# Soft mixture of experts by nested fast matrix products: more pairs split a third time

## The chip, the cores and the metric

The kernel runs on one core of one Trainium2 chip. The metric is the device time of one execution in microseconds (us); lower is better. The time before is the median of three runs. The profile is of one more execution, taken by the hardware profiler.

## The reference

```python
x: (16, 512, 512)   router_logits: (16, 512, 8)   expert_weights: (8, 512, 2048)   all float32
probs = softmax(router_logits, axis=-1)
output = zeros((16, 512, 2048))
for e in range(8):
    output += probs[:, :, e:e+1] * matmul(x, expert_weights[e])
```

With the probabilities multiplied into x this is one product of an 8192 x 4096 matrix (tokens by expert and hidden index) and a 4096 x 2048 matrix (the weights).

## The kernel before

**The products.** The big product is cut 2 x 2 x 2 and made by Winograd's form of Strassen's scheme, with seven products instead of eight; the code calls them P1 to P7 (`right[r]`, `lefts[r, q]`, `products[r, q]`). P1 takes the first four experts' weights and the first half of the output columns (`b11`), P2 the last four experts' (`b21`); the right sides of P3 to P7 are sums of weights. Rows come in 16 blocks q of two times 256. Each `Product` is cut once more in the same way, into seven steps in the order `STEPS = (1, 5, 6, 2, 7, 3, 4)`. A step is eight matmuls of 128 x 128 by 128 x 512 (f16 into a PSUM bank of f32). Its inputs are, on the left, `z` (x times a probability, made by VectorE; halves 0 and 1 of the inner index), `s2` (pool `d`) and the inner `i`; on the right blocks of weights (1, 2, 3) and sums of them (5, 6, 7, 4), tiles of pool `w`. After a step `post` takes its bank: P1's results go by ScalarE copies and VectorE adds to `kept` in DRAM; P2 fetches these as a base into a tile of pool `h`, and VectorE adds the bank to it at every step but step 2.

**The split.** `Split` and `Third` cut steps 1 and 5 of a pair of products (a and b, two neighbouring row blocks) a third time. The two steps of both products would be 4 x 8 = 32 matmuls of 512 columns; as a third level they are 2 x 7 parts (named x1 to x7 for step 1, q1 to q7 for step 5) of four matmuls of 256 columns, 56 in all. For it VectorE makes four sums S of the lefts for each pair (`Third.queue_sums`, tile `s`: 128 x 1024), eight sums `t` of the weights once for each r (`Split.queue`; 128 x 1024), and adds halves of banks after parts 6 and 7 (128 x 256). ScalarE copies half of a bank after part 5, and the other half into `t5`. x5 needs the first sum S0, x6 S1, and so on.

**The stages.** `stages` is a list of one or two products that TensorE works through step by step, a and b in turn; a stage of two has 14 slots. Stages 0 to 5 are P1's pairs (q = 2 to 13), stages 6 and 7 hold one product of P2 and one of P1, stages 8 to 14 are P2's pairs, and stage 15 (`k5`) begins P5. Before stage 0 a first phase makes P1's rows q = 0 and 1 directly: for two column halves n, four experts e, four chunks c and four row parts j it runs one matmul each, with weights as they land; `early_z0` and `early_xp1` make its inputs and those of stage 0 by matmuls with a diagonal, and `keep_p` stores all probabilities in `p_dram`. Where the next stage is split, the last two slots (step 4 of a and b) are held and run between its parts (`held`, `run_third`): x1 x5 q1 q5, a held slot, x2 q2 x6 q6, the other, x7 q7 x3 q3 x4 q4.

**The order.** Each engine runs in the order in which the program names its work (`keep_in_program_order`). VectorE's work that nobody needs at once lies in `queue` as `Task`s with costs. `slack()`, called at each slot, adds 1.73 us to TensorE's planned clock and runs tasks while VectorE's planned clock is at least 0.3 us behind; `need(task)` runs the queue up to a task that a step requires, wherever it stands; `evacuated()` adds what `post` costs. A stage's own inners come into the queue when it starts (`queue_i`), the next stage's lefts, S, s2 after its first slot (`queue_lefts`). Hooks (`at(stage, slot, ...)`) start the rest: `fetch_at` the bases on SyncE's queue, `wedge_at` the casts and three sums that prepare later right sides (12 and 22), `odd_t` and `sums_at` more of these. `start_loads(stage + 2)` puts the next but one stage's `xT` and `pT` on SyncE's queue after slot 1, or after the slot that `late` names. Stores of results go by GpSimd's queue, weights that return from DRAM (`fetch_w`) by ScalarE's.

**The pools.** `w` has 15 tiles, `z` 8, `x` 9, `h` 13, `d` 3, PSUM 8 banks. A tile is handed out again when its last reader is done; a DMA or an engine that writes into it waits for that.

Before the change stages 2 to 5 and 9 are split, and six of P3's. The weight sums `t` of P1 are queued in stage 1, those of P2 in stage 8.

Of the kernel before, what the change touches and what calls it, by code (L numbers as in the profile page):

```python
# [31 lines left out]
def kernel(  # L32
# [7 lines left out]
    nc = tc.nc  # L40
    P = 128
# [35 lines left out]
    def half():  # L77
        return h_tile([P, NB], f32)
# [32 lines left out]
    def tt(o, a, b, op):  # L111
        dve(nc.vector.tensor_tensor(out=o, in0=a, in1=b, op=op))  # L112
# [9 lines left out]
    def sp(o, i):  # L122
        note(nc.sync.dma_start(out=o, in_=i))
# [7 lines left out]
    def mm(ps, z, w, start, stop):  # L131
        note(nc.tensor.matmul(ps, z, w, start=start, stop=stop, skip_group_check=True))  # L132
# [3 lines left out]
    def new_w():  # L136
        return wpool.tile([P, K8, NB], f16, name="w", tag="w")
# [31 lines left out]
    def inner_sums(b, t7=None):  # L169

        w = {1: b[0, 0], 2: b[1, 0], 3: b[1, 1], 7: t7 or b[0, 1]}

        def step(p, x, y):
            if p not in w:
                w[p] = new_w()
            tt(w[p], x, y, SUB)
        return w, {5: lambda: step(5, b[0, 1], b[0, 0]), 6: lambda: step(6, b[1, 1], w[5]),
                   4: lambda: step(4, b[1, 0], w[6]), 7: lambda: step(7, b[1, 1], b[0, 1])}
# [39 lines left out]
    def early_p(t):  # L218
        if t == 0:
            return softmax(lg0[t], 4, cpool.tile([P, HE, 4], f16, name="ph0"))  # L220
        pf = softmax(lg0[t], 4, cpool.tile([P, HE, 4], f32, name="pf0"))
        odd = pf.rearrange("p e (q j) -> p e q j", j=2)[:, :, :, 1]
        tt(odd[:, 0:2], odd[:, 0:2], odd[:, 2:4], ADD)
        ph = cpool.tile([P, HE, 4], f16, name="ph1")
        dve(nc.vector.tensor_copy(ph, pf))
        return ph
# [16 lines left out]
    def diag_e(e):  # L243
        return diag(ph0[0][:, e].unsqueeze(2))

    def early_z0(e, d, js=range(4)):
        for j in js:
            ps = bank()
            for c in range(C):
                mm(ps[:, ds(c * P, P)], xs0[:, j, ds(c * P, P)], d[:, j], c == 0, c == C - 1)  # L250
            evacuate(z0[j][:, e], ps.rearrange("p (c t) -> p c t", c=C), j)
# [8 lines left out]
    def early_xp1(j, d):  # L260
# [6 lines left out]
        mm(ps, ones, d.rearrange("p e t -> p (e t)"), True, True)  # L267
        evacuate(xp1[t][1][:, :, rows], ps.rearrange("p (e t) -> p e t", e=HE), 1)

    R = 4  # L270
    J = HQ // R
    p_dram = dram.tile([NHQ, 3 * HE, HQ], f16, name="p_dram")
# [32 lines left out]
                for c in (2 * g, 2 * g + 1) for j in (2 * h, 2 * h + 1)]  # L305
    ORDERS = [(c, j) for c in range(C) for j in range(4)], QUARTERS

    ds_ = [diag_e(0)]
    early_z0(0, ds_[0], (0, 1))
    for i in range(3):  # L310
# [4 lines left out]
    for e in (1, 2):  # L315
        ds_.append(diag_e(e + 1))
        early_z0(e, ds_[e])
    for n in range(2):
        ps = [bank() for _ in range(4)]
        for e in range(HE):  # L320
            if n == 0 and e == 1:
                early_z0(3, ds_[3])
                ph0.append(early_p(1))
                ds_ = [diag_j(j) for j in range(4, 8)]
                keep_p = softmax_of_all()
                w, sums = inner_sums(b11, new_w())
            for c, j in ORDERS[n == 0 and e == 0]:
                mm(ps[j], z0[j][:, e, c], b11[e // 2, n][:, e % 2 * C + c, :],
                   e + c == 0, e == HE - 1 and c == C - 1)
            if n == 1:  # L330
                for j in ((4, 5), (6, 7), (), ())[e]:
                    early_xp1(j, ds_[j - 4])
                if e == 1:
                    sums[5]()
        for j in range(4):
            o = half()
            act(nc.scalar.copy(o, ps[j]))
            sp(kept[j // 2][n].rearrange("(p j) m -> j p m", j=2)[j % 2], o)
        if n == 0:
            keep_p()  # L340

    ordered[0] = True
# [247 lines left out]


    THIRD = (1, 5)
    COLS = [ds(i * HQ, HQ) for i in range(2)]

    class Split:

# [8 lines left out]

        def make(self, p, i):
            if i == 0:
                self.t[p] = wpool.tile([P, 4, C, HQ], f16, name="t", tag="w")
            w, t = self.right.op(p), self.t[p]
            block = lambda k, n: w[:, ds(k * C, C), COLS[n]]  # L610
            x, y = ((block(0, 1), block(0, 0)), (block(1, 1), t[:, 0]), (block(1, 1), block(0, 1)),
                    (block(1, 0), t[:, 1]))[i]
            tt(t[:, i], x, y, SUB)

        def op(self, p, m):
            if m in (1, 2, 3):
                k, n = ((0, 0), (1, 0), (1, 1))[m - 1]
                return self.right.op(p)[:, ds(k * C, C), COLS[n]]
            i = {5: 0, 6: 1, 7: 2, 4: 3}[m]
            need(self.task[p, i])  # L620
            return self.t[p][:, i]

    class Third:
# [25 lines left out]
        def part(self, p, m):  # L649
            n = "xq"[THIRD.index(p)]  # L650
            if m == 1:
                self.b.banks[n] = bank()
            ya, yb = self.a.banks.get(n), self.b.banks[n]
            z, w = self.op(p, m), self.split.op(p, m)
            o = {1: (yb, 0), 5: (yb, 1), 2: (ya, 0), 6: (yb, 0), 7: (yb, 0), 3: (ya, 1), 4: (yb, 0)}[m]
            for c in range(C):
                mm(o[0][:, COLS[o[1]]], z[:, c], w[:, c], m == 1 and c == 0, c == C - 1)
            clock["pe"] += 0.44
            if m == 5:
                ya = self.a.banks[n] = bank()  # L660
                act(nc.scalar.copy(ya[:, COLS[0]], yb[:, COLS[0]]))
                self.t5[n] = h_tile([P, HQ], f32)
                act(nc.scalar.copy(self.t5[n], yb[:, COLS[1]]))
            elif m in (6, 7):
                evacuated(0.35)
                tt((ya if m == 6 else yb)[:, COLS[1]], yb[:, COLS[0]], self.t5[n], ADD)

# [262 lines left out]
    for q in range(1, 13, 2):  # L930
        add(product(3, q), product(3, q + 1))
    end = add(product(3, 13))
    late[k3 - 1] = 6

    for k, q in ((k7, 14), (k7 + 1, 15)):
        at(k - 1, 6, lambda q=q: queue_into(lefts[7, q]))
# [76 lines left out]
    sums_at(5, 8, 2, b21, (7,))  # L1013
    sums_at(5, 12, 2, b21, (4,))
    for i, (kn, e) in enumerate((kn, e) for kn in ((0, 0), (1, 0), (1, 1)) for e in range(2)):
        wedge_at(4 + i, 2, kn, e, (4 + i, 11))

    def fetch_at_w(stage, slot, of, what, kn):
        at(stage, slot, lambda: of.__setitem__(kn, fetch_w(what, kn)))
# [43 lines left out]
    last2 = k5 - 1  # L1063
    for stage, slot, q in ((9, 9, 12), (10, 2, 11), (10, 9, 22), (last2, 8, 21)):
        at(stage, slot, lambda q=q: cast_odd(q))
    at(11, 6, odd_t)
    for i, kn in enumerate(((0, 0), (1, 1), (1, 0))):
        fetch_at_w(11 + (8 + 4 * i) // 14, (8 + 4 * i) % 14, t1, "t1", kn)
        fetch_at_w(last2, 2 + 2 * i, t2, "t2", kn)
    sums_at(12, 8, 5, t1, (5, 6))  # L1070
    sums_at(13, 2, 5, t1, (7, 4))
    sums_at(last2, 9, 6, t2, (5, 6))
    at(k5, 4, odd_t4)
    sums_at(k5, 5, 6, t2, (7, 4))
# [141 lines left out]
            post(p)  # L1216
    finish.step, finish.post = step_at_end, post_at_end

    for stage in (2, 3, 4, 5):
        third(stage, 1)  # L1220
    at(1, 2, splits[1].queue)
    for stage in (9, ):
        third(stage, 2)
    at(8, 2, splits[2].queue)

    for q in KEEP:
        for k, slot in enumerate((1, 5)):
# [3 lines left out]
        third(stage, 3)  # L1231
    at(k3, 9, splits[3].queue)

    need_first = [right[1].task[p] for p in (6, 7, 4)]
    for p in (2, 3):
        lefts[1, p].queue_make(0)
    queue.append(need_first[0])
    for p in (2, 3):
        lefts[1, p].queue_s2()
    for p in (2, 3):  # L1240
        lefts[1, p].queue_make(1)
    queue.extend(need_first[1:])
    start_loads(1)
    store_loads(0)
    finish_loads(1)
# [30 lines left out]
```

## Time and profile before

| What | Value |
|---|---|
| Median of three runs | 1366.98 us (1366.88 to 1367.12) |
| Profiled execution, its own time | 1367.07 us |
| Its span, first to last instruction | 1365.1 us |
| Granted TensorE clock | 1.000 |
| TensorE (PE) busy | 1359.9 us, 100% |
| VectorE (DVE) busy | 1126.5 us, 83% |
| GpSimd (POOL) busy | 407.0 us, 30% |
| ScalarE (ACT) busy | 195.7 us, 14% |
| DMA | 356.41 MB, mean 261 GB/s |

The profile's rows read so: engine, line of the code, operation, the tile written `<-` the tiles read, sizes, and a count; a timeline row begins with its start and its length in us, and ends with the engine's idle time before it and who ended it. A row of a stretch of time gives for each engine its busy time (and instructions), then the granted clock, the share of the DMA engines and GB/s. Most calls pass through helpers: line 132 is every matmul, 112 every VectorE tensor-tensor operation, 123 SyncE's DMAs and 126 GpSimd's, so that rows are told apart by their tiles. Matmuls overlap, so their mean duration (375 ns) is longer than their spacing.

### The profile page before, as it was taken

The page shows a single profiled execution, that of the slowest core. Times are in us where ns is not written, and L with a number is a line of the kernel's source. Part 1 is how long each engine was busy: PE and PEld are TensorE (multiplying, and loading weights), DVE is VectorE, ACT ScalarE, POOL GpSimd, SP SyncE. Part 2 cuts the span into 40 slices and gives each one's busy share as a digit, 9 for nine tenths or more (in the row PEclk, how much of TensorE's full clock was granted, in tenths as well). Part 3 has the DMA queues.
Part 4 walks back from the last instruction along what each step waited for, and adds up shares of the span by engine and source line. Part 5 has one row for each costly group of instructions (what it writes and reads, how often), then busy time and mean ns, then how long its engine had stood idle before and what let it go on. Part 6 is the DMA issues. An engine that isn't in the chain of part 4 may idle for free.

```text
span 1365.1 us, 18194 instructions
## 1 busy us (share of the span) xinstructions
PE 1359.9 (100%) x6657; PEld 648.7 (48%) x6657; DVE 1126.5 (83%) x1367; ACT 195.7 (14%) x362; POOL 407.0 (30%) x644
## 2 busy tenths in 40 slices
PE   9999999999999999999999999999999999999998
PEld 4455544544444444444444444444444444456554
DVE  5975787989789788788887888888889797998873
ACT  3232311100011111111111100000000000123221
POOL 3123333331223342333322122242332422223232
PEclk9999999999999999999999999999999999999999
DMA  9999999999898999999999978989898979999896
GB/s 195 242 218 228 253 242 323 310 300 383 257 304 268 311 350 274 293 279 292 328 258 331 344 247 221 216 240 203 232 252 220 252 203 292 302 217 245 196 206 119
DMA packets 193385, 356.41 MB, mean 261 GB/s; under 512 B 53136, under 2 KB 87184, under 8 KB 188176
## 3 DMA queue, kind: packets, MB, share of 16 engines
q0 software_dynamic: 88048, 183.02, 55.3%
q1 hardware_dynamic: 99488, 132.25, 31.9%
q10 hardware_dynamic: 5760, 39.99, 7.6%
q8 instruction: 52, 0.85, 0.2%
q14 instruction: 37, 0.30, 0.1%
HBM read 214.47 MB, written 167.97 MB: 280 GB/s over the span
## 4 chain that ended last, share of the span: by engine, by line
PE 99%; DMA 0%; DVE 0%; issue 0%; ACT 0%; POOLq 0%
PE ps L132 99%; DMA w<-in_x_dram 0%; DVE z L238 0%; DVE h L112 0%; ACT h L1213 0%; POOLq L1260 0%
## 5 line engine op out<-in xcount | busy, mean ns | idle before, releaser
L132 PE MATMUL ps<-w,z 128*128 128x512 f16 x5240 | 1125.7, 375 | 0.0
L132 PEld LDWEIGHTS <-z 128*128 128x128 f16 x5328 | 521.2, 98 | 598.4
L126 POOL DMA_DIRECT2D out_dram<-h x380 | 249.3, 662 | 736.5 <-ACT h L582 352.6
L112 DVE TENSOR_TENSOR h<-ps,h 128x512 f32<-128x512 f32 x415 | 284.6, 687 | 184.7 <-PE ps L132 166.7
L112 DVE TENSOR_TENSOR z<-xT,pT 128x2048 f16<-128x2048 f16 x216 | 261.9, 1217 | 0.0
L132 PE MATMUL ps<-w,d 128*128 128x512 f16 x880 | 199.1, 379 | 0.0
L132 PEld LDWEIGHTS <-d 128*128 128x128 f16 x880 | 86.1, 98 | 101.5
L112 DVE TENSOR_TENSOR z<-z,d 128x2048 f16<-128x2048 f16 x110 | 131.7, 1217 | 0.0
L582 ACT COPY h<-ps 128x512 f32<-128x512 f32 x64 | 37.5, 585 | 524.5 <-PE ps L132 521.1
L112 DVE TENSOR_TENSOR w<-w 128x1024 f16<-128x1024 f16 (+2 forms) x88 | 100.0, 1146 | 1.8 <-PE ps L132 1.0
L571 ACT COPY h<-ps 128x512 f32<-128x512 f32 x90 | 52.7, 585 | 293.5 <-PE ps L132 264.1
L112 DVE TENSOR_TENSOR ps<-ps,h 128x512 f32<-128x512 f32 (+1 forms) x110 | 64.0, 585 | 26.0 <-PE ps L132 25.7
L112 DVE TENSOR_TENSOR d<-z 128x1024 f16<-128x1024 f16 x110 | 74.6, 687 | 5.1 <-PE ps L132 3.6
L568 ACT COPY h<-ps 128x512 f32<-128x512 f32 x90 | 51.8, 589 | 132.4 <-PE ps L132 129.6
L126 POOL DMA_DIRECT2D kept<-h x56 | 30.8, 549 | 110.9 <-ACT h L571 78.0
L126 POOL DMA_DIRECT2D wd<-w x78 | 44.2, 592 | 35.0 <-DVE w L112 27.5
L126 POOL DMA_DIRECT2D w<-in_expert_weights_dram x65 | 48.6, 778 | 19.5 <-issue 13.8
L112 DVE TENSOR_TENSOR u<-xT,pT 128x2048 f16<-128x2048 f16 x38 | 46.2, 1217 | 0.0
L112 DVE TENSOR_TENSOR h<-h 128x512 f32<-128x512 f32 (+2 forms) x69 | 45.1, 675 | 0.1
L112 DVE TENSOR_TENSOR z<-z,u 128x2048 f16<-128x2048 f16 x34 | 41.3, 1216 | 0.1
L112 DVE TENSOR_TENSOR z<-z 128x2048 f16<-128x2048 f16 x32 | 39.1, 1222 | 0.7
L564 ACT COPY ps<-ps 128x512 f32<-128x512 f32 x45 | 25.6, 570 | 94.4 <-PE ps L132 87.2
(61 smaller groups left out, 291.9 us busy)
## 6 DMA issues: line engine op xcount, KB each, us to landing
out_dram<-h POOLq DMA_DIRECT2D x380, 256.0 KB, 6.8
pT<-p_dram SPq DMA_DIRECT2D x125, 256.0 KB, 6.3
h<-kept SPq DMA_DIRECT2D x116, 256.0 KB, 6.7
w<-wd ACTq DMA_DIRECT2D x25, 1024.0 KB, 9.0
xT<-x SPq DMA_DIRECT2D x76, 256.0 KB, 6.8
w<-in_expert_weights_dram POOLq DMA_DIRECT2D x35, 512.0 KB, 10.9
wd<-w POOLq DMA_DIRECT2D x64, 256.0 KB, 6.6
h<-out_dram SPq DMA_DIRECT2D x60, 256.0 KB, 5.4
```

The lines of the kernel that those rows point to most:

```text
L112: dve(nc.vector.tensor_tensor(out=o, in0=a, in1=b, op=op))
L126: note(nc.gpsimd.dma_start(out=o, in_=i, **how))
L132: note(nc.tensor.matmul(ps, z, w, start=start, stop=stop, skip_group_check=True))
L564: act(nc.scalar.copy(self.banks["b"], x))
L568: act(nc.scalar.copy(o[tn], q if p == 5 else x))
L571: act(nc.scalar.copy(o[TN[p]], b if p == 2 else x))
L582: act(nc.scalar.copy(o[tn], b))
```

## The change

- **First phase and stages 0 and 1.** All six stages of P1 (0 to 5) are split. The sums `t` for step 1 are made in the first phase (`early_thirds(1, ...)`: the first before its matmuls, three after expert 0), those for step 5 right after sum 5, one expert earlier than sum 5 stood (`early_thirds(5)`, at e = 0 of n = 1). Of the first phase's last 16 matmuls, chunks 2 and 3 (four each) are held and run between the parts of stage 0, where a held slot would be; the copies and `kept` stores of n = 1 follow there (`first_results`).
- **Start of the queue.** Lefts of a and b, S of stage 0 and sum 6 are run before stage 0; then s2, the second lefts and sum 7 are queued, and sum 4 behind the inners.
- **P2.** Stages 8 to 12 are split instead of stage 9 alone, with `t` queued in stage 7. The loads that stages 8 to 11 start (for stages 10 to 13) come after slot 13 and no longer after slot 1.
- **Moved.** The last wedge's sums from stage 9 slot 11 to stage 10 slot 6; `odd_t` from stage 11 slot 6 to stage 12 slot 5; the `t1` sums from stages 12 and 13 to 13 and 14.
- **t5.** Its two halves share one tile of pool `d` instead of two of pool `h`.

```diff
+    def third_weights(w, t, i):
+        block = lambda k, n: w[:, ds(k * C, C), COLS[n]]
+        x, y = ((block(0, 1), block(0, 0)), (block(1, 1), t[:, 0]), (block(1, 1), block(0, 1)),
+                (block(1, 0), t[:, 1]))[i]
+        tt(t[:, i], x, y, SUB)
+    def new_t():
+        return wpool.tile([P, 4, C, HQ], f16, name="t", tag="w")
+    early_t = {}
+    def early_thirds(p, some=range(4)):
+        if p not in early_t:
+            early_t[p] = new_t()
+        for i in some:
+            third_weights(w[p], early_t[p], i)
...
+    def first_product(ps, n, e, c, j):
+        mm(ps[j], z0[j][:, e, c], b11[e // 2, n][:, e % 2 * C + c, :],
+           e + c == 0, e == HE - 1 and c == C - 1)
+    def first_results(ps, n):
+        for j in range(4):
+            o = half()
+            act(nc.scalar.copy(o, ps[j]))
+            sp(kept[j // 2][n].rearrange("(p j) m -> j p m", j=2)[j % 2], o)
...
     for e in (1, 2):
         ds_.append(diag_e(e + 1))
         early_z0(e, ds_[e])
+    w, sums = inner_sums(b11, new_w())
+    early_thirds(1, (0,))
     for n in range(2):
         ps = [bank() for _ in range(4)]
         for e in range(HE):
             if n == 0 and e == 1:
                 early_z0(3, ds_[3])
+                early_thirds(1, (1, 2, 3))
                 ph0.append(early_p(1))
                 ds_ = [diag_j(j) for j in range(4, 8)]
                 keep_p = softmax_of_all()
-                w, sums = inner_sums(b11, new_w())
             for c, j in ORDERS[n == 0 and e == 0]:
-                mm(ps[j], z0[j][:, e, c], b11[e // 2, n][:, e % 2 * C + c, :],
-                   e + c == 0, e == HE - 1 and c == C - 1)
+                if n == 0 or e < HE - 1 or c < 2:
+                    first_product(ps, n, e, c, j)
             if n == 1:
                 for j in ((4, 5), (6, 7), (), ())[e]:
                     early_xp1(j, ds_[j - 4])
-                if e == 1:
+                if e == 0:
                     sums[5]()
-        for j in range(4):
-            o = half()
-            act(nc.scalar.copy(o, ps[j]))
-            sp(kept[j // 2][n].rearrange("(p j) m -> j p m", j=2)[j % 2], o)
+                    early_thirds(5)
         if n == 0:
+            first_results(ps, n)
             keep_p()
...
             i = {5: 0, 6: 1, 7: 2, 4: 3}[m]
-            need(self.task[p, i])
+            need(self.task.get((p, i)))
...
                 act(nc.scalar.copy(ya[:, COLS[0]], yb[:, COLS[0]]))
-                self.t5[n] = h_tile([P, HQ], f32)
+                if not self.t5:
+                    t = spool.tile([P, 2, HQ], f32, name="d", tag="d")
+                    self.t5 = {"x": t[:, 0], "q": t[:, 1]}
                 act(nc.scalar.copy(self.t5[n], yb[:, COLS[1]]))
...
-    late[k3 - 1] = 6
+    late.update({k3 - 1: 6, 8:13,9:13,10:13,11:13})
...
-        wedge_at(4 + i, 2, kn, e, (4 + i, 11))
+        wedge_at(4 + i, 2, kn, e, {5:(10,6)}.get(i, (4 + i, 11)))
...
-    at(11, 6, odd_t)
+    at(12,5, odd_t)
...
-    sums_at(12, 8, 5, t1, (5, 6))
-    sums_at(13, 2, 5, t1, (7, 4))
+    sums_at(13,8, 5, t1, (5, 6))
+    sums_at(14,2, 5, t1, (7, 4))
...
-    for stage in (2, 3, 4, 5):
+    for stage in (0,1,2,3,4,5):
         third(stage, 1)
-    at(1, 2, splits[1].queue)
-    for stage in (9, ):
+    splits[1].t = early_t
+    for stage in (8,9,10,11,12):
         third(stage, 2)
-    at(8, 2, splits[2].queue)
+    at(7,2, splits[2].queue)
...
+    def last_first(c):
+        for j in range(4):
+            first_product(ps, 1, HE - 1, c, j)
+        if c == C - 1:
+            first_results(ps, 1)
+    for c in (2, 3):
+        held.append(lambda c=c: last_first(c))
     need_first = [right[1].task[p] for p in (6, 7, 4)]
     for p in (2, 3):
         lefts[1, p].queue_make(0)
+    thirds[0].queue_sums()
     queue.append(need_first[0])
+    flush(need_first[0])
+    clock["dve"] = 0.0
     for p in (2, 3):
         lefts[1, p].queue_s2()
     for p in (2, 3):
         lefts[1, p].queue_make(1)
-    queue.extend(need_first[1:])
+    queue.append(need_first[1])
+    at(0, 0, lambda: queue.append(need_first[2]))
```

More of the change, by code (lines that the diff above doesn't have):

```diff
@@ L268, in early_xp1 @@
         evacuate(xp1[t][1][:, :, rows], ps.rearrange("p (e t) -> p e t", e=HE), 1)
+    COLS = [ds(i * HQ, HQ) for i in range(2)]
+    def third_weights(w, t, i):
[11 more added lines that the diff above has]
+            third_weights(w[p], early_t[p], i)
     R = 4
@@ L592 @@
     THIRD = (1, 5)
-    COLS = [ds(i * HQ, HQ) for i in range(2)]
     class Split:
@@ L607, in make @@
             if i == 0:
[L608 to L613, printed above, removed]
+                self.t[p] = new_t()
+            third_weights(self.right.op(p), self.t[p], i)
         def op(self, p, m):
```

## The prediction

> **What bounds the kernel now.** I read the page first, then the chain that ended last, then TensorE's timeline in the first stages, then the table of stretches by stage, then VectorE's groups and timeline, and last the DMA view of narrow stretches.
>
> ```profile
> span 1365.1 us, 18194 instructions
> PE 1359.9 (100%) x6657; PEld 648.7 (48%) x6657; DVE 1126.5 (83%) x1367; ACT 195.7 (14%) x362; POOL 407.0 (30%) x644
> 9.30 1352.25 PE ps L132 x6612
> 47.38 3.62 PE L132 MATMUL ps<-w,d 128*128 128x512 f16 x16
> 50.84 20.88 PE L132 MATMUL ps<-w,z 128*128 128x512 f16 x96
> 71.56 3.62 PE L132 MATMUL ps<-w,d 128*128 128x512 f16 x16
> 93.19 1.04 PE L132 MATMUL ps<-w,s 128*128 128x256 f16 x8
> 94.06 1.04 PE L132 MATMUL ps<-t,z 128*128 128x256 f16 x8
> 94.94 3.62 PE L132 MATMUL ps<-w,d 128*128 128x512 f16 x16
> ```
>
> The chain is one TensorE piece from 9.30 us to the last copy: TensorE never waits after the start, so only fewer or cheaper matmuls can win, and every wait that is added counts in full. Busy times overlap, so I take spacings: 16 matmuls of 512 columns from 47.38 to 50.84 are 216 ns each, 8 of 256 columns from 93.19 to 94.06 are 109 ns each. VectorE, at 83%, is next in line.
>
> **The saving.** A split pair replaces the 32 wide matmuls of its products 1 and 5 with 56 narrow ones: 32 x 0.216 = 6.91 us become 56 x 0.109 = 6.10, so 0.81 saved. The rows agree: from step 6 of stage 0 to step 6 of stage 1 (neither split) are 71.56 - 47.38 = 24.18, on to step 6 of split stage 2 are 94.94 - 71.56 = 23.38. The Trainium skill (TensorE: Matmul & The Clock Gate, Back-to-back issue gap) says that in a real stream the spacing is set by the weight load too, 81 ns at 128 columns and 131 ns at 512. Interpolated to about 98 ns at 256, an estimate, a split would cost 56 x 98 - 32 x 131 ns = 1.3 us; the trace's 109 and 216 ns contradict it. Six more stages are split (0, 1, 8, 10, 11, 12): -4.85 us if nothing waits.
>
> **The first phase.** Eight sums `t` for products 1 and 5 now come from VectorE before stage 0.
>
> ```profile
> 14.08 1.29 DVE L238 CAST z<-ps 128x512 f16<-128x512 f32 x2 [1.84 <-PE ps L132]
> 28.78 1.29 DVE L238 CAST xT<-ps 128x512 f16<-128x512 f32 x2 [3.72 <-PE ps L132]
> 33.12 1.29 DVE L238 CAST xT<-ps 128x512 f16<-128x512 f32 x2 [3.04 <-PE ps L132]
> 33.57 13.98 PE L132 MATMUL ps<-w,z 128*128 128x512 f16 x64
> 34.44 2.29 DVE L112 TENSOR_TENSOR w<-w 128x4096 f16<-128x4096 f16 x1
> 36.65 2.35 DVE L112 TENSOR_TENSOR z<-xT,pT 128x2048 f16<-128x2048 f16 x2
> 40.03 2.05 ACT L337 COPY h<-ps 128x512 f32<-128x512 f32 x4 [5.62 <-PE ps L132]
> 42.61 1.12 SPq L123 DMA_DIRECT2D pT<-p_dram  x2
> ```
>
> The first (0.69, about 0.61 in a row) fits in the 1.84 us of idling before 14.08. The next three push the softmaxes by 1.9 us; the 3.72 us before 28.78 take that up. If that cover were gone, the casts at 28.78, and no matmul, would be late. The copy to `p_dram` starts 0.7 us later and its first reader stands at 42.61. Nothing for TensorE.
>
> From 30.1 VectorE is a solid row: sum 5 (2.2), four `t` (2.5), the casts that stood at 33.12 (to 36.1), lefts a, b (2.3), S0 to S3 of stage 0 (2.5; S0 done at 39.2), sum 6 (to 43.1). TensorE: e = 2 and 3 begin at 33.57 and would end 32 x 0.216 later, at 40.48; with 8 matmuls held, x1 of stage 0 starts at 38.75 and x5, which needs S0, at 39.19. So 0 to 0.1 us there. Stage 0's split plus held blocks take 6.10 + 1.73, to 46.58; its eight slots of 1.73 end at 60.40. ScalarE's four copies (2.05) start 0.45 before the last held block ends at 43.97 and end at 45.6; the copy of a's bank (0.57) ends at 46.2, before slot a6 at 46.58. Cover 0.4 us, counted as nothing. The `kept` stores now queue on SyncE behind stage 1's transposes and two `pT` of stage 2: four `h` buffers are held longer, nobody reads them here.
>
> **Stage 0 into 1: a new wait.** VectorE still owes s2 a, s2 b, left 1 of a and b, sum 7, both inners and sum 4 (10.2 us) and starts them at 45.5, after the add of q7. Row by row: s2 to 46.7, lefts to 49.0, sum 7 to 51.2, inners to 53.5, sum 4 to 55.7. Each is in time (a7 needs sum 7 and an inner at 53.50). The planner's clocks give the order after that. From TensorE 6.16 each slot adds 1.73 and steps are popped while VectorE is 0.3 behind: a6 pops to 7.91, b6 to 11.25, a2 nothing, b2 to 13.63, a7 sum 4 to 15.83 (eviction 16.44), b7 nothing (17.15), a3 left A of stage 1 (18.29; 18.90), b3 left B (20.04; 20.65). S0 of stage 1 is never popped; x5 demands it, so it stands behind the eviction of b3.
>
> ```profile
> 85.64 0.69 DVE L112 TENSOR_TENSOR h<-ps,h 128x512 f32<-128x512 f32 x1 [1.03 <-PE ps L132]
> 85.81 0.60 PE L132 MATMUL ps<-t,s 128*128 128x256 f16 x4
> 95.71 0.69 DVE L112 TENSOR_TENSOR s<-s,z 128x1024 f16<-128x1024 f16 x1
> 96.43 1.29 DVE L112 TENSOR_TENSOR s<-z,s 128x1024 f16<-128x1024 f16 x2
> ```
>
> At stage 2, x5 runs at 85.81, so b3 ended at 85.37 and its eviction began 0.27 later; S stood ready long before. In the changed stage 1: b3 ends 60.40, eviction 60.67 (next step 0.61 later), S0 61.28 to 61.97, seen at about 62.05; x5 was due at 60.84. TensorE waits **1.2 us**. The bound below is 0 (S0 before the eviction), above 1.6 (the ScalarE cover gone too). S1 to S3 follow while held a4 runs.
>
> **Stage 7.** It must now also make S of stage 8 (4) and eight `t`: 12 x 0.61 = 7.3 us.
>
> ```profile
> 206.50:230.70 24.20, 24.20 (x114) 10.95 (x113) 16.76 (x20) 3.50 (x6) 8.22 (x15) 1.00 1.13 297
> 222.26 0.69 DVE L112 TENSOR_TENSOR h<-ps,h 128x512 f32<-128x512 f32 x1 [4.48 <-PE ps L132]
> 326.70:350.90 24.20, 24.20 (x114) 10.97 (x112) 20.06 (x22) 1.17 (x2) 4.32 (x8) 1.00 1.01 369
> L112 DVE TENSOR_TENSOR w<-w 128x4096 f16<-128x4096 f16 x20 | 45.5, 2286 | 1.1 <-PE ps L132 1.0
> L112 DVE TENSOR_TENSOR w<-w 128x2048 f16<-128x2048 f16 x16 | 19.5, 1218 | 0.1
> L112 DVE TENSOR_TENSOR ps<-ps,h 128x256 f32<-128x256 f32 x4 | 1.7, 433 | 2.4 <-PE ps L132 2.4
> ```
>
> VectorE idles 24.20 - 16.76 = 7.4 us in stage 7, 4.48 of it in one piece, and its wedge steps (3 x 1.22) come in the queue behind these: they slide into stage 8. Nothing, but nothing is left over either.
>
> **Stages 8 to 12.** Stage 12 has 20.06 us of VectorE, two of it sums of 2.29 that move to stage 13: 15.5. A split adds 4 x 0.69 and 4 x 0.43: 20.0 of 23.38, so 3.4 spare. Wedge steps (3.65) fall into 8, 9 and 11 and take that; but steps in a row overlap by 0.08 (two of 1.22 in 2.35), some 25 of them, so about 2 us stay spare there. S is queued right behind the first lefts, early in the stage before, so it is not the last here as it is in stage 0, which owes 10 us at its start. I put 0.2 us on the tight spots (first x5, the adds of x6 to q7 when an eviction stands ahead of them); bounds 0 and 0.43, one add, in each of six stages. The odd sums and `t1` sums move to stages 12 to 14; there S of a next split is not owed.
>
> What must land: base (0,1) of a stage goes into the `h` buffer of the stage before, freed by the store of its (0,0).
>
> ```profile
> out_dram<-h POOLq DMA_DIRECT2D x1, 256.0 KB, 13.6
> h<-kept SPq DMA_DIRECT2D x1, 256.0 KB, 5.9
> out_dram<-h POOLq DMA_DIRECT2D x1, 256.0 KB, 5.4
> h<-kept SPq DMA_DIRECT2D x1, 256.0 KB, 14.8
> out_dram<-h POOLq DMA_DIRECT2D x18, 256.0 KB, 12.5
> h<-kept SPq DMA_DIRECT2D x16, 256.0 KB, 9.9
> ```
>
> The first four are this very pair before stages 11 and 12 (stores at 291.4 and 315.6, fetches at 305.0 and 321.0): 19.5 and 20.2 us together. From the end of a2 to the end of b6 one stage later are 7 slots, 6.10 and 2 slots, 21.7 us (22.5 without a split); less about 0.9 for copy and issue, 20.8 remain. It holds by 0.6 to 1.3. The loads of two stages on (`xT`, `pT`) are now queued behind these bases on SyncE, so a late store delays them too; VectorE waits for both with evictions behind. Before, the bases stood behind the loads, which wait for `x` buffers; that wait goes. The `t5` halves leave `h` for the third `d` buffer, free once the stage before has done b6.
>
> **Sum.** The profiled execution took 1367.07 us (span 1365.1 and 2.0 around it; the median of the runs is 1366.98): 1367.07 - 4.85 + 1.2 + 0.2 = **1363.6**.
>
> **Rivals.** *No new wait* (S0 ready): 1362.2. For it: stages 2 to 5 show none; against: there sums 4 and 7 and s2 aren't owed. 0.08. *Bases late a little*: the slower store and a median fetch, 13.6 + 9.9 = 23.5, are 2.7 over the 20.8; 10 and 12 absorb it in their 3.4, 9 and 11 lose 0.7 each: 1365.0, and up to the edge of the next case. For it: the medians sum to 22.4, over the 20.8 too; against: the two pairs themselves, and less traffic ahead of the bases. 0.28. *Slower: VectorE becomes the bound in stages 8 to 12*: if store and base take 26 us together, 5.2 late, stages 9 and 11 lose 3.2 each and 10 and 12 1.8 each: 10 us, 1373.6; the time is slower than before by 0.2% from 25.3 us on (2 x 2.5 + 2 x 1.1 = 7 us lost). For it: single landings of 13.6 and 14.8, and VectorE nearly full; against: they didn't coincide. 0.17. *Narrow matmuls dearer:* the groups' busy time
>
> ```profile
> L132 PE MATMUL ps<-t,s 128*128 128x256 f16 x264 | 36.0, 273 | 0.0
> ```
>
> over count is 136 ns; 56 x 0.136 - 6.91 = +0.7 a pair, 1371.3. The page's rule above points the same way. The spacing of 109 ns speaks against both. 0.02.
>
> **The numbers.** Forecast 0.45. A measurement of this kernel tells about 0.2% (2.7 us) from no change. Faster: 0.45 + 0.08; same: 0.28, and 0.02 of the slower case's lower edge; slower: the rest. The range runs from just under no wait, 1362.0, over the late bases to the edge of the slower case, 1369.5.
>
> **What would show it.** 336 more narrow matmuls at a spacing of 109 ns; a TensorE gap of 1.2 us near 61 us in front of `ps<-t,s`, ended by VectorE's `s`; split stages of 23.4 us from 225 to 345. Wrong if VectorE idles for `h<-kept` or `xT` there and TensorE's gaps follow it, or if there is no gap at 61.

## The result and the profile after

The changed kernel takes 1378.2 us (median of 4 runs, 1376.4 to 1380.1) where the kernel before takes 1367.05 beside it: a ratio of 1.0081, 95% interval 1.0069 to 1.0093. That is 11.2 us slower; 3.4 us faster was forecast, and 1369.5 was the upper end of the range. The profiled execution took 1378.16 us. Its page, first its span, then the engines, then the chain that ended last by engine:

```profile
span 1376.4 us, 18550 instructions
...
PE 1358.8 (99%) x6801; PEld 661.2 (48%) x6801; DVE 1149.0 (83%) x1415; ACT 203.3 (15%) x386; POOL 407.1 (30%) x644
...
PE 77%; DMA 9%; issue 8%; POOL 3%; DVE 2%; SPq 0%; POOLq 0%; ACT 0%; DVEq 0%
```

The chain was one TensorE piece before and now has 281 pieces, and transfers hold 9% of it. The busy shares of VectorE and DMA say little about this; the idle times in front of single instructions do. TensorE's timeline shows where it waits (start, duration, engine, operation; in brackets the idle time before it and what ended it):

```profile
40.58 0.61 PE L132 MATMUL ps<-t,s 128*128 128x256 f16 x4 [1.23 <-DVE s L112]
...
63.44 0.61 PE L132 MATMUL ps<-t,s 128*128 128x256 f16 x4 [1.03 <-DVE s L112]
...
118.67 1.03 PE L132 MATMUL ps<-t,z 128*128 128x256 f16 x8
119.54 3.62 PE L132 MATMUL ps<-w,d 128*128 128x512 f16 x16
...
143.26 1.03 PE L132 MATMUL ps<-t,z 128*128 128x256 f16 x8 [1.06 <-DVE ps L112]
...
163.11 4.24 PE L132 MATMUL ps<-w,z 128*128 128x512 f16 x16 [3.25 <-DVE h L112]
...
229.18 1.02 PE L132 MATMUL ps<-w,z 128*128 128x512 f16 x4 [1.35 <-DVE h L112]
...
334.88 1.17 PE L132 MATMUL ps<-w,z 128*128 128x256 f16 x8 [0.71 <-ACT ps L685]
...
348.97 3.20 PE L132 MATMUL ps<-w,z 128*128 128x512 f16 x14 [2.53 <-DVE z L112]
```

Counted from start to start over the usual spacing, the waits are 1.40 us (stage 0), 1.20 (stage 1), 0.2, 1.22 and 3.42 with 1.6 more at a halved clock (stages 3 to 5), 1.51 and 0.9 (stages 7 and 8), 1.0 and 2.69 (stage 12), and 1.0 in small ones later: 16.1 us. With the 4.85 saved that makes +11.3, against a measured difference of 11.2 us. So the saving came, and three times as much went into waits. VectorE's timeline shows where it stood ahead of them:

```profile
117.05 1.23 DVE L112 TENSOR_TENSOR z<-xT,pT 128x2048 f16<-128x2048 f16 x1 [1.35 <-DMA xT<-xs]
...
141.64 1.23 DVE L112 TENSOR_TENSOR z<-xT,pT 128x2048 f16<-128x2048 f16 x1 [2.37 <-DMA xT<-xs]
...
154.91 1.23 DVE L112 TENSOR_TENSOR z<-xT,pT 128x2048 f16<-128x2048 f16 x1 [11.37 <-issue]
...
225.17 0.69 DVE L112 TENSOR_TENSOR s<-z 128x1024 f16<-128x1024 f16 x1 [4.01 <-DMA wd<-w]
...
347.09 0.69 DVE L112 TENSOR_TENSOR h<-ps,h 128x512 f32<-128x512 f32 x1 [4.25 <-DMA h<-kept]
```

These are late transposed x blocks in P1, a `w` tile that a store still held in stage 7, and a late base in stage 12. For the third row the profile names no releaser, but the transposed block that it reads landed at 154.83 us, 0.08 before it started. (Runs of kernels with gaps of several us scatter, by up to 7 us, so each gap below is read from the one profiled execution, and each time is a median.)

### The profile page after: what moved, and what is told of

It reads as the page before. It is cut to its first block, busy times and chain, and to the rows that moved or that the text cites. A ratio compares the mean times of both kernels' runs of the same rounds, so it can differ in the third digit from the quotient of the medians.

```text
span 1376.4 us, 18550 instructions
## 1 busy us (share of the span) xinstructions
PE 1358.8 (99%) x6801; PEld 661.2 (48%) x6801; DVE 1149.0 (83%) x1415; ACT 203.3 (15%) x386; POOL 407.1 (30%) x644
## 4 chain that ended last, share of the span: by engine, by line
PE 77%; DMA 9%; issue 8%; POOL 3%; DVE 2%; SPq 0%; POOLq 0%; ACT 0%; DVEq 0%
PE ps L132 77%; DMA kept<-h 2%; DMA out_dram<-h 2%; DMA w<-in_x_dram 1%; DMA xT<-xs 1%; DMA h<-kept 1%; POOL out_dram L126 1%; DMA w<-in_expert_weights_dram 1%; DVE z L112 1%; POOL w L126 1%; DMA wd<-w 1%; DMA xs<-in_x_dram 1%; POOL kept L126 1%; DVE h L112 1%; DVE t L112 0%
## 5 line engine op out<-in xcount | busy, mean ns | idle before, releaser
L132 PE MATMUL ps<-w,z 128*128 128x512 f16 x5144 | 1100.7, 374 | 8.0 <-DVE h L112 4.6
L132 PEld LDWEIGHTS <-z 128*128 128x128 f16 x5280 | 515.8, 98 | 590.3 <-issue 10.4
L132 PEld LDWEIGHTS <-s 128*128 128x128 f16 x544 | 53.0, 98 | 13.8 <-DVE s L112 2.8
L132 PE MATMUL ps<-t,s 128*128 128x256 f16 x408 | 55.7, 273 | 3.1 <-DVE s L112 2.3
L112 DVE TENSOR_TENSOR ps<-ps,d 128x256 f32<-128x256 f32 x68 | 28.1, 429 | 25.6 <-PE ps L132 25.5
L112 DVE TENSOR_TENSOR ps<-ps,h 128x512 f32<-128x512 f32 (+1 forms) x66 | 45.1, 687 | 4.4 <-PE ps L132 4.1
```

## Experiments

**The two halves apart.** First P1's part alone, with these lines as they were in P2; then P2's part alone on the kernel before (t5 in one `d` tile in both).

```
-    for stage in (8,9,10,11,12):      # and late, wedge, odd_t, sums_at, splits[2].queue
+    for stage in (9,):                # as before
```

> Stages 0 to 5 split as after, P2 as before (stage 9 alone split, the hooks and the loads in their old places). Theory (P1's waits are P1's own: the S0 waits 1.40 and 1.20 and some 6.4 us of late xT in stages 3 to 6): 1367.0 - 2 x 0.81 + 9 = about 1374.5, with the same three groups of TensorE gaps near 39, 62 and 118 to 165 us. Rival (VectorE's load in stages 8 to 12 is what makes the change slow, and P1's gaps are partly recovered): 1368 or less.

> P1 as before (stages 2 to 5 split), P2 as after (stages 8 to 12 split, moved hooks, loads behind bases; t5 in one d tile). Theory (P2's waits are its own: the w tile for S of stage 8, 2.4 us, ScalarE's fetch of t1, 1.0 us, the late base of stage 12, 2.8 us): 1367.0 - 4 x 0.81 + 6.2 = about 1370. Rival 1 (these waits are inherited from the shift that P1 gives): 1363.8. Rival 2 (VectorE's load is the bound in stages 8 to 12): over 1372, with gaps in every one of these stages.

Measured: P1's part 1373.25 us (ratio 1.0045, 1.0031 to 1.0058), P2's part 1367.99 (1.0004, 0.9995 to 1.0014). P1's part keeps its gaps (1.40 near 39, 1.19 near 62, 0.4 to 4.8 from 118 to 159 us; its profiled execution, 1377.28, stands 4 us over its median). P2's part has only one gap of size, 3.2 us in stage 12, and with the saving of four more splits it breaks even: my expectation of 1370 was too high. VectorE stood here:

```profile
337.18 0.69 DVE L112 TENSOR_TENSOR h<-ps,h 128x512 f32<-128x512 f32 x1 [4.80 <-DMA h<-kept]
```

By the medians the excess of the two, 6.1 and 0.8 us, doesn't add up to the whole 11.2. By the profiled executions, 10.2 and 0.6 against 11.1, it nearly does. P1's six runs lie between 1371.1 and 1377.3, so it isn't shown that the parts disturb each other. The wait for a `w` tile, 2.4 us in the changed kernel, costs TensorE 0.4 in P2's part.

**P1: what makes xT late.** Three edits, each on P1's part alone: stage 1 not split; a tenth x buffer for one `h` buffer; the expert casts moved from slot 2 to slot 8.

```
-    for stage in (0,1,2,3,4,5):
+    for stage in (0,2,3,4,5):                                   # first
-    xpool = ctx.enter_context(tc.tile_pool(name="xpool", bufs=9))
-    hpool = ctx.enter_context(tc.tile_pool(name="hpool", bufs=13))
+    xpool = ctx.enter_context(tc.tile_pool(name="xpool", bufs=10))   # second
+    hpool = ctx.enter_context(tc.tile_pool(name="hpool", bufs=12))
-        at(i + 1, 2, lambda kn=kn: cast21(kn))
+        at(i + 1, 8, lambda kn=kn: cast21(kn))                  # third
```

> As p1_only, but stage 1 is not split (stages 0 and 2 to 5 are). Theory (stage 1's split makes its second lefts some 11 us later, holds x buffers that the loads of stage 3 wait for, and sets the late rhythm of xT): the gaps of 1.2 at 62 us and of 118 to 165 us go, the 1.4 near 39 stays: 1367.0 - 0.81 + 1.4 = 1367.6. Rival (the split of stage 0, or the first phase's new order, delays the loads): the gaps of 118 to 165 us stay, about 1373.

> As p1_only, with ten x buffers in place of nine and twelve h buffers in place of thirteen. Theory (xs waits for an x buffer): the gaps of 118 to 165 us go, 1367.0 - 1.62 + 2.6 = 1368.0, unless the missing h buffer makes a wait of its own. Rival (the transposes are slow because of the casts and stores that they share the DMA queues with, not because they start late): 1374.5, as p1_only.

> As p1_only, with P1's four blocks of expert casts (one a stage, stages 1 to 4) issued at slot 8 of their stage in place of slot 2, so that they don't stand between the x loads and the transposes. Theory (the loop x load, transposes, next x load takes 26 us because the transposes land behind casts and stores that were issued ahead of them): the gaps of 118 to 165 us go in most part, 1367 to 1369. Rival (the loop is long by its own steps, whatever shares the queues; only another x buffer helps): 1373.

Measured: 1368.14 (1.0004, 0.9995 to 1.0013), 1370.59 (1.0028, 1.0015 to 1.0040) and 1368.14 (1.0010, 1.0001 to 1.0019). Each takes the xT gaps away; the second leaves one of 1.8 us near 163, where VectorE waited 4.94 us for casts. GpSimd's timeline shows the issues of the x loads, in the order: before, changed, stage 1 unsplit, casts moved:

```profile
66.26 1.48 POOL L126 DMA_DIRECT2D xs<-in_x_dram  x2
87.18 0.71 POOL L126 DMA_DIRECT2D xs<-in_x_dram  x1
...
110.54 1.45 POOL L126 DMA_DIRECT2D xs<-in_x_dram  x2
```
```profile
72.89 0.74 POOL L126 DMA_DIRECT2D xs<-in_x_dram  x1 [8.55 <-DVE z L112]
95.41 0.71 POOL L126 DMA_DIRECT2D xs<-in_x_dram  x1 [7.24 <-DMA xT<-xs]
...
121.37 1.45 POOL L126 DMA_DIRECT2D xs<-in_x_dram  x2 [9.82 <-DMA xT<-xs]
```
```profile
67.49 1.47 POOL L126 DMA_DIRECT2D xs<-in_x_dram  x2
88.39 0.72 POOL L126 DMA_DIRECT2D xs<-in_x_dram  x1
...
111.78 1.46 POOL L126 DMA_DIRECT2D xs<-in_x_dram  x2
```
```profile
96.27 0.72 POOL L126 DMA_DIRECT2D xs<-in_x_dram  x1 [8.10 <-DMA xT<-xs]
...
119.21 1.45 POOL L126 DMA_DIRECT2D xs<-in_x_dram  x2 [7.66 <-DMA xT<-xs]
```

Stage 1's split puts its S ahead of its second lefts (`z`), so these come later, and only they free the x buffers: GpSimd stands 8.55 us in front of the second x load for stage 3, which goes out at 72.89 and not right behind the first, as the pair at 66.26 does in the kernel before; the casts and `kept` stores queued behind it wait too. From there the loop x load, transposes, next x load runs on buffers alone: 26.0 us from one stage to the next (95.41 to 121.37) against a TensorE stage of 23.4, while before (87.18 to 110.54) and without stage 1's split (88.39 to 111.78) it ran with the stages, at 23.4. With the casts moved it takes 22.9 (96.27 to 119.21), less than a stage, and a late start no longer grows. The DMA view of the first two transposes of stage 4 (changed, then before; median us from issue to landing) shows a part of the 26:

```profile
xT<-xs SPq DMA_TRANSPOSE x2, 11.6
```
```profile
xT<-xs SPq DMA_TRANSPOSE x2, 8.2
```

With the casts moved, it is the second two that stand behind them:

```profile
xT<-xs SPq DMA_TRANSPOSE x2, 10.1
```

There the first x load takes 4.7 us in place of 8.6, the first two transposes 5.5 in place of 11.6, and the second two 10.1 in place of 2.5. So the transposes as a whole aren't quicker, but the first two, which the next stage's first lefts need, have landed at 107.5 and not at 117.0. Both theories were right in part: the delay starts at the x buffers, and it persists and grows because the casts are on their way together with the x loads and the first transposes. What the stores add wasn't tested.

**The first phase.** P1's part without stage 1's split, with TensorE's matmuls held in the written order in the second half of the first phase.

```
     for n in range(2):
+        ordered[0] = n == 1
```

> As p1_no1 (stages 0 and 2 to 5 split, P2 as before), with TensorE's order held as written from the first phase's second half on. Theory (the 1.4 us before stage 0's S products come from TensorE's matmuls being put in another order there, which makes the x and p blocks and so the lefts later): the gap near 39 us falls to 0.3 or less, 1368.1 - 1.3 = 1366.8. Rival (VectorE's t sums, not TensorE's order, make S0 late): the gap stays, 1368.1.

Measured: 1367.33 (1.0002, 0.9993 to 1.0011). The changed kernel's TensorE, then its VectorE:

```profile
29.36 0.39 PE L132 MATMUL ps<-ident,w 128*128 128x128 f16 x4
...
30.75 2.10 PE L132 MATMUL ps<-w,z 128*128 128x512 f16 x9
```
```profile
31.38 2.29 DVE L112 TENSOR_TENSOR w<-w 128x4096 f16<-128x4096 f16 x1
...
39.83 0.69 DVE L112 TENSOR_TENSOR s<-z 128x1024 f16<-128x1024 f16 x1
```

The same two views with the order held:

```profile
28.31 0.39 PE L132 MATMUL ps<-ident,w 128*128 128x128 f16 x4
...
29.48 0.38 PE L132 MATMUL ps<-h,ones 128*128 128x512 f16 x1 [0.34 <-DVE xT L238]
...
39.64 0.60 PE L132 MATMUL ps<-t,s 128*128 128x256 f16 x4
```
```profile
30.06 2.29 DVE L112 TENSOR_TENSOR w<-w 128x4096 f16<-128x4096 f16 x1
...
38.50 0.69 DVE L112 TENSOR_TENSOR s<-z 128x1024 f16<-128x1024 f16 x1
```

In the changed kernel five other matmuls had been put ahead of the `ident` matmuls (69 of them run in a row before, with the order held 64), so VectorE's casts, sum 5 and S0 came 1.3 us later. In written order sum 5 starts at 30.06 and S0 at 38.50, no S product waits, and 0.5 us is lost once near 29.

**P2: the late base.** On P2's part alone: the three fetches of `t1` a stage later; stage 12 not split; stage 12's fourth bases ahead of the loads of stage 13.

```
-        fetch_at_w(11 + (8 + 4 * i) // 14, (8 + 4 * i) % 14, t1, "t1", kn)
+        fetch_at_w(12 + (8 + 4 * i) // 14, (8 + 4 * i) % 14, t1, "t1", kn)   # first
-    for stage in (8,9,10,11,12):
+    for stage in (8,9,10,11):                                                     # second
-    fetch_at(k if tn == (1, 0) else k - 1, 3 if tn == (1, 0) else slot, bases[2, q], tn)
+    fetch_at(*((k, 3) if tn == (1, 0) and k != 12 else (k - 1, min(slot, 12))), bases[2, q], tn)   # third
```

> As p2_only, with ScalarE's three fetches of t1 one stage later. Theory (the base of stage 12 was issued at 319.08 us and landed at 337.06, because the DMA queues have a backlog of some 15 us there, and the t1 fetches of 321.71 and 328.36 share them with it): the base lands earlier by one to two of these fetches, the gap of 3.2 us near 335.6 goes in most part, 1364.5 to 1365.5. Rival (the loads of xT and pT ahead of it on SP's queue make it late): the gap stays over 2 us, 1367 to 1368.

> As p2_only, with stages 8 to 11 split and stage 12 not. Theory (only stage 12's bases are late): 1368.0 + 0.8 - 3.2 = 1365.6. Rival (the DMA backlog makes the next stage's base late whether it is split or not): about 1368.5, with a gap of the same size in stage 12 or 13.

> As p2_only, with the fourth base of each of stage 12's two products fetched at slot 12 of stage 11, ahead of stage 13's x and p loads on SP's queue, in place of slot 3 of stage 12, behind them. Theory (the base that landed at 337.06 us stood behind four loads that were issued from 314.46 on, and landed between 328 and 336): the gap of 3.2 us near 335.6 goes, 1364.3 to 1365. Rival (the backlog of the DMA queues, not the order on SP, is the limit, as the run without stage 12's split suggests with its 5 us wait for a p load): the wait passes to the loads of stage 13, which are then behind the bases, about 1367 to 1368.

Measured: 1368.84 (1.0011, 1.0002 to 1.0021), 1372.09 (1.0038, 1.0023 to 1.0053), 1369.30 (1.0017, 1.0007 to 1.0026). None got faster; each time the wait only moved. Without the fetches nothing waits near 335, so the theory holds for that gap, but a gap of 3.0 us stands near 424. Without stage 12's split the late transfer is a p block, now behind the bases (8.43 us of VectorE, 5.0 of TensorE). With the bases first, the p block is late too (VectorE 2.90 us for a base, then 4.18 for `pT`), and a gap of 3.0 stands near 427:

```profile
337.63 1.22 DVE L112 TENSOR_TENSOR z<-xT,pT 128x2048 f16<-128x2048 f16 x1 [8.43 <-DMA pT<-p_dram]
```
```profile
336.01 0.69 DVE L112 TENSOR_TENSOR h<-ps,h 128x512 f32<-128x512 f32 x1 [2.90 <-DMA h<-kept]
...
344.89 1.23 DVE L112 TENSOR_TENSOR z<-xT,pT 128x2048 f16<-128x2048 f16 x1 [4.18 <-DMA pT<-p_dram]
```

The rival, a backlog of the DMA queues whatever their order, fits. The traces show where it comes from: SyncE's and ScalarE's DMAs share eight semaphores (GpSimd's have eight more), and in every kernel here each of the 1181 DMAs that reuse one was issued only after the DMA before it on that semaphore had landed. So at most eight of SyncE and ScalarE together are on their way, and the late base of the changed kernel, landed at 346.97, was issued at 332.08, 0.4 us after an earlier base had landed. In the kernel before, the DMA share (the second last column) is 1.02 from 160 to 369 us, though with 0.95 behind it the share alone doesn't tell where a wait will be. The later gap is VectorE's; its busy time (the column DVE) over the same 61 us, before and with the bases first:

```profile
160.00:369.00 209.00, 209.00 (x1014) 99.00 (x1012) 180.60 (x206) 21.55 (x39) 61.11 (x105) 1.00 1.02 297
369.00:430.00 61.00, 61.00 (x285) 27.62 (x283) 51.91 (x56) 6.99 (x12) 15.05 (x27) 1.00 0.95 298
```
```profile
369.00:430.00 61.00, 58.60 (x272) 26.42 (x271) 60.86 (x60) 6.99 (x12) 15.43 (x27) 1.00 0.92 297
```

The moved hooks (odd sums and `t1` sums a stage later) fill VectorE from 346 us on; what it waits for earlier is then missing at 427. P2's part alone has the same 60.86 us there and no such gap, so a full VectorE alone makes no gap; it can't make up what was lost ahead of it. The reading was tested by taking the hooks back, on top of the third edit:

```
-    wedge_at(4 + i, 2, kn, e, {5:(10,6)}.get(i, (4 + i, 11)))
+    wedge_at(4 + i, 2, kn, e, (4 + i, 11))
-    at(12,5, odd_t)
+    at(11, 6, odd_t)
-    sums_at(13,8, 5, t1, (5, 6))
-    sums_at(14,2, 5, t1, (7, 4))
+    sums_at(12, 8, 5, t1, (5, 6))
+    sums_at(13, 2, 5, t1, (7, 4))
```

> As p2_base, with the wedge's go-on, the odd block's t sums and the four t1 sums back in the places that they have in the kernel before (9,11; 11,6; 12,8; 13,2). Theory (VectorE is the bound from 346 to 430 us, where it was busy 60.9 of 61 us, because these hooks were moved into it out of stages 9 to 12): the gap of 3.0 us near 427 us goes, 1369.3 - 3.5 = 1366. Rival (the work can't be done earlier, since the transfers that it waits for land late, or VectorE has no room in stages 9 to 12 either): gaps of the same sum appear in stages 11 to 13, 1369 or more.

Measured: 1372.61 (1.0039, 1.0025 to 1.0053). The gap near 427 is gone, as the theory has it, but gaps of 1.03 us near 290 and 4.2 near 338 stand in its place: the rival's number. In front of the second, VectorE works from 327.85 us on without a wait over 0.3 us, three sums of 2.3 us among its work: it has no room for these sums there either.

**Stage 7's w tile.** The changed kernel with the casts at slot 8; then the changed kernel with stage 8 not split (its `t` sums queued at (8, 2)).

```
-        at(i + 1, 2, lambda kn=kn: cast21(kn))
+        at(i + 1, 8, lambda kn=kn: cast21(kn))      # first
-    for stage in (8,9,10,11,12):
+    for stage in (9,10,11,12):                      # second
```

> The changed kernel with one edit: P1's expert casts at slot 8 in place of slot 2 of stages 1 to 4. Theory (the late xT of stages 3 to 6 come from the order of casts and transposes, and the w wait of 2.4 us in stage 7 is handed on from that delay): gaps left are 1.4 near 39, 1.2 near 62 and some 3.2 in stage 12, 1367.0 - 4.85 + 5.8 = 1368. Rival (the w wait of stage 7 is its own): 2.4 more, 1370.4.

> The changed kernel with stages 9 to 12 split in P2 and not stage 8, its t sums queued a stage later. Theory (stage 7's TensorE gaps of 1.5 and 0.9 us come from S of stage 8, which takes a w tile that a store still holds): no gap between 215 and 245 us; 1378.2 + 0.8 - 2.4 = 1376.6. Rival (the w tiles are short there anyhow): a gap of 1.5 us or more stays in stage 7 or 8.

Measured: 1372.76 (1.0048, 1.0030 to 1.0066) and 1374.67 (1.0051, 1.0036 to 1.0066). With the casts moved, the xT gaps go, but stage 7's wait grows to 3.75 us: it isn't handed on from the late xT, and that theory falls. Without stage 8's split TensorE is busy through stages 7 and 8:

```profile
215.00:245.00 30.00, 30.00 (x141) 13.62 (x140) 22.77 (x26) 3.56 (x7) 10.82 (x18) 1.00 1.11 326
```

So the split of stage 8 asks for a `w` tile that a store (`wd<-w`) still holds. In all nine kernels with that split S waits for it, for 2.3 to 4.0 us of VectorE; what TensorE loses in stages 7 and 8 differs: nothing at 2.30 and 2.62, 0.4 at 3.22 (P2's part alone), 1.0 at 3.82, 2.4 at 4.01 (the changed kernel), 3.75 and a halved clock at 3.85. So up to 2.6 us of this wait cost nothing there; above that it reaches TensorE.

**The mends together.** Casts at slot 8, written order, fourth bases first; then the same without stage 1's split.

> The changed kernel with three edits: the casts at slot 8, TensorE's order held as written in the first phase's second half, the fourth bases of stage 12 ahead of stage 13's loads. If the causes named so far are all: gaps left are 0.5 in the first phase and 1.2 near 62, 1367.0 - 4.85 + 1.7 = 1363.9. Rival (base fix only moves the wait): 1367.

> As after_fixed, but stage 1 is not split. Theory: the saving of 0.81 goes and so does the wait of 1.2 near 62 us: 1363.5, 0.4 faster than after_fixed. Rival (the wait of 1.2 passes to stage 2 in another form): 1364.7.

Measured: 1371.46 (1.0038, 1.0025 to 1.0050) and 1372.83 (1.0036, 1.0023 to 1.0048). Both theories miss, by 8 and 9 us: P1 now has only 0.5 and 1.2 us of gaps (0.5 without stage 1's split), but the first has 1.9 us in stages 7 and 8, and from 335 to 430 us there are 3.8 and 6.4 us, 3.0 of them at 427 with a halved clock behind. None of these orders mends P2's part.

**Fewer splits.** The kernel before (t5 in one `d` tile in all four) with stages 9 and 10; with 9 to 11 and the loads behind the bases; that with the sixth wedge's stores at (10, 6), as in the change; and that with stage 0 split, the casts moved and written order.

```
-    for stage in (9, ):
+    for stage in (9,10):                                        # first
+    for stage in (9,10,11):                                     # the others
+    late.update({k3 - 1: 6, 8:13, 9:13, 10:13})
-    wedge_at(4 + i, 2, kn, e, (4 + i, 11))
+    wedge_at(4 + i, 2, kn, e, {5:(10,6)}.get(i, (4 + i, 11)))   # third, fourth
```

> The kernel before with stage 10 split beside stage 9 and t5 in one d tile; hooks and loads in their old places. Theory (one more split stage adds VectorE work that its idle time holds, and no transfer becomes late): 1367.0 - 0.8 = 1366.2. Rival (the backlog of the DMA queues makes a base late as soon as two stages in a row are split): 1367.5 or more.

> The kernel before with stages 9 to 11 split, the loads of stages 10 to 12 behind the bases (slot 13 of stages 8 to 10), t5 in one d tile; hooks in their old places. Theory (two more split stages fit into VectorE's idle time): 1367.0 - 1.6 = 1365.4. Rival (late p loads or bases in stage 12, as in the run without stage 12's split): a gap of 2 us or more there, 1368 or more.

> As p2_9_11_late (stages 9 to 11 split, loads of stages 10 to 12 behind the bases), with the sixth wedge's sums and stores at (10, 6) in place of (9, 11), as the changed kernel has it. Theory (the 1.0 us near 290 us is a base behind that wedge's stores): the gap goes, 1366.3 - 1.0 = 1365.3. Rival (the stores a stage later make a base or a p load of stage 11 or 12 late): a gap of 1 us or more near 310 to 340, 1366.3 or more.

> The last kernel's P2, and in P1 the split of stage 0 beside stages 2 to 5, with the casts at slot 8 and TensorE's order held in the first phase's second half. Theory (a saving of 0.8 against a wait of 0.5 near 29 us): 1365.0, and no gap over 0.3 us after it. Rival (the earlier clock of P1 shifts P2's stores and bases so that a late base comes back): 1366.5 or more.

Measured: 1374.18 (1.0050, 1.0038 to 1.0063), 1366.32 (0.9997, 0.9988 to 1.0006), 1365.45 (0.9983, 0.9974 to 0.9993) and 1365.57 (0.9986, 0.9977 to 0.9995). One more split with the loads ahead of the bases costs 7 us, one base being late by 4.2 us in front of VectorE:

```profile
290.22 0.69 DVE L112 TENSOR_TENSOR h<-ps,h 128x512 f32<-128x512 f32 x1 [4.23 <-DMA h<-kept]
...
296.22 1.03 PE L132 MATMUL ps<-w,z 128*128 128x512 f16 x2 [4.82 <-DVE z L112]
```

With the loads behind them and the wedge's stores a stage later, two more splits are free of waits: the page of the third kernel gives TensorE back the chain.

```profile
span 1363.9 us, 18311 instructions
...
PE 99%; DVE 0%; issue 0%; ACT 0%; DVEq 0%
```

The third and fourth are faster than the kernel before, by 0.17% and 0.14% with intervals clear of 1, and faster than the changed one; they don't differ from each other. Splits of 9 to 11 with the loads ahead of the bases weren't tried.

## Why the prediction was wrong

The term that failed is the one for new waits: the sum had 1.2 + 0.2 us, and the profile has 16.1. The rows of the sum, one by one:

- **Price and saving: right.** Eight matmuls of 256 columns take 119.54 - 118.67 = 0.87 us, 109 ns each, and -4.85 closes the sum of the gaps to 0.2 us. The rival of dearer narrow matmuls falls.
- **Stage 0 into 1: right.** 1.2 us forecast near 61, 1.20 measured near 62, in front of `ps<-t,s` and ended by VectorE's `s`, which runs right behind the add of slot b3's bank, as forecast. With stage 1's saving of 0.8 it makes that split a loss by itself.
- **The first phase: a step failed.** "So 0 to 0.1 us there" took TensorE's written order for granted. The order is free until the first phase ends; with it held, sum 5 starts at 30.06 (30.1 forecast) and S0 at 38.50 (done at 39.2 forecast). The difference was 1.4 us.
- **P1's stages 3 to 5: a step is missing.** The prediction followed the second lefts of stage 0 and found each in time. It did not follow those of stage 1, which come at 71.37 us in the changed kernel, behind S and s2, nor what they release. They free x buffers, and the loads for stage 3 stand behind that on GpSimd's queue, with casts and stores behind them. It cost 6.4 us here, the largest item.
- **Stage 7: a step failed.** "Nothing, but nothing is left over either" counted VectorE's time alone. S of stage 8 also needs a `w` tile; it and its aftermath cost 2.4 us.
- **Stages 8 to 12: partly right.** VectorE's time in stages 9 to 11 did suffice (20.6 to 20.8 us of 23 busy in the changed kernel), and two more splits there are free. "It holds by 0.6 to 1.3" failed in stage 12: the bound from two store and fetch pairs was made with the transfers' times of before, but transfers were already at a DMA share of 1.02, so what shifts in time makes another one late: 2.69 us, and 1.0 by ScalarE standing at a fetch, with 10.07 us of idling before the copy behind it. What that fetch waited for last is the semaphore that a base used until it landed at 334.00; the store that it also waited for had landed at 329.75. So this too was a wait for a base.

The first of these rows is the fetch on ScalarE's queue, the second the copy behind it:

```profile
334.10 0.33 ACTq L166 DMA_DIRECT2D w<-wd  x1
334.47 0.36 ACT L685 COPY ps<-ps 128x256 f32<-128x256 f32 x1 [10.07 <-PE ps L132]
```

- **The hooks moved to stages 12 to 14: a step failed.** "There S of a next split is not owed" was true, but VectorE is full there: 60.86 of 61 us against 51.91. It costs nothing to speak of in the changed kernel (0.2 us near 436, with as full a VectorE), and 3 us in the four kernels that changed the order of stage 12's bases or of the `t1` fetches and kept these hooks.
- **The rivals.** The one on the slower side named late bases with VectorE nearly full; the mechanism exists, in stage 12 instead of four stages, and the sign that the prediction set for being wrong was met (4.25 us before `h<-ps,h` at 347.09). Its price at the edge doesn't fit: 2 x 2.5 + 2 x 1.1 are 7.2 us and would give 1370.8, 0.3% above the kernel before and not 0.2%; nothing else hangs on it. The loss in P1's stages 3 to 5 and in stage 7 had no rival at all.

What stays open: why six of the kernels, the changed one among them, have 0.8 to 1.2 us of gaps between 1170 and 1230 us that others with the same P3 don't have, and whether P1's and P2's parts cost more together than apart: 4 us by the medians, 0.3 by the profiled executions.

## What to carry over

An operation that is made later is late for its readers and also for whoever waits for the buffers that it releases: follow both, through every entry queued behind that wait. Where transfers already fill the DMA queues, a landing time of before is no constant; count loads, stores and tiles per stage as a resource beside the engines' times, and expect a mended wait to reappear at the next one. Splitting only the stages with room (9 to 11) gave 0.17%; splitting six stages more than before cost 0.8%.

## What the hardware showed

A TensorE gap can cost more than its length. The granted clock (third column from the end) in the 3.2 us after the gap of 3.42, and after that of 5.0 in P2's part without stage 12's split:

```profile
163.00:166.20 3.20, 3.09 (x8) 1.16 (x8) 3.20 (x6) 0.00 (x0) 2.14 (x4) 0.51 1.12 381
```
```profile
343.50:349.00 5.50, 5.42 (x13) 1.93 (x13) 5.47 (x6) 0.00 (x0) 0.00 (x0) 0.50 1.05 372
```

The matmuls there start 427 ns apart, not 216. All seven gaps of 3.4 us or more in these kernels were followed by this; of the seven between 2.5 and 3.3, those of 2.55, 2.98 (two of three) and 3.04 were, and those of 2.69 and 3.23 not. It cost 1.2 to 2.8 us on top of the gap. Two of the P2 kernels have the same gap near 425 us: the one with the bases first runs at full speed behind it, the one with the later `t1` fetches at half speed:

```profile
430.42 1.89 PE L132 MATMUL ps<-w,d 128*128 128x512 f16 x8 [2.82 <-DVE ps L112]
```
```profile
427.23 3.50 PE L132 MATMUL ps<-w,d 128*128 128x512 f16 x8 [2.88 <-DVE ps L112]
```

The Trainium skill (TensorE: Matmul & The Clock Gate, Part 1: The HAM clock gate) has the clock halved after an idle window of about 3.4 us, in windows that run freely and not from the gap's start. The rows agree for the longer gaps and in that the same gap was answered in two ways; that gaps of 2.55 to 3.04 us were enough in some runs does not agree.
